# The MLP norm's factors by ScalarE's root and a Newton step, the input differences made inside the output projection, and that projection in finer steps of heads and tiles

## The chip, the cores and the metric

The kernel runs on one core of a Trainium2 chip. The metric is the device time of one execution in microseconds; the value shown is the median of three runs.

## The reference, cut to what matters

Four pre-norm residual layers on a stream of 16 learned meta positions and 512 frames, width 1024. Layer 0 and layer 3 mix tokens with a gated DeltaNet of 8 heads, layer 1 with differential attention of 8 heads, layer 2 with a Griffin RG-LRU block; each mixer ends in an output projection, and each layer is followed by a squared-ReLU MLP of inner width 4096:

```python
def rmsnorm(x, w):
    y = x * lax.rsqrt(jnp.mean(x * x, axis=-1, keepdims=True) + EPS)
    return y * w

def sq_relu_mlp(u, w1, w2):
    return jnp.square(jax.nn.relu(u @ w1)) @ w2

for layer in range(DEPTH):
    u = rmsnorm(h, norm_mix_w[layer])
    y = mixer(u)                      # heads' outputs o, then o @ w_out
    h = h + keep * y
    u = rmsnorm(h, norm_mlp_w[layer])
    h = h + keep * sq_relu_mlp(u, mlp_w1[layer], mlp_w2[layer])
```

## The kernel before, in words

The stream is kept transposed: eight tiles `h[0]` to `h[7]` of 128 features by 528 positions (512 positions from the last layer's output projection on). Every product of large matrices is made as three passes: a weight is split into `hi` and `lo`, an activation into `hi` and `lo`, and TensorE adds `hi·hi`, `hi·lo` and `lo·hi` in PSUM. Such a product runs over two halves of the positions (264 or 256 columns), so one 128 by 128 block of weights costs six matmuls. PSUM tiles come from two pools, `d` with three buffers and `c` with five.

**Weights.** They are streamed in units of eight blocks. `unit()` pops the next unit and prepares further ones: ScalarE casts `hi` (L305) and writes its negative to `lo` (L309), then a DMA that GpSimd issues (L310) adds the raw weights from memory to `lo`. The split tiles rotate through seven buffers.

**Background work.** The heads of a mixer are Python generators (`dn_core` and `dn_gate`, `da_core`) that are advanced between matmuls by `tick()`, by a hand-kept model time `self.now`; `drain(g, ...)` advances the model until these generators are done. The instructions so written are then ordered on each engine by the framework's own scheduler; each engine runs its order strictly, and waits at an instruction whose inputs are not there.

**Output projection** (`out_proj`, from L600). It multiplies the heads' outputs by `w_out` and adds the result into `h[d]` on VectorE (L612). For the DeltaNet and the attention it is called twice: once for heads 0 to 3 over all eight tiles `d`, then, after all heads are drained, for heads 4 to 7 over all eight tiles. In the second call every tile `d` is followed by `mlp_prep(d)`: ScalarE scales it by the norm's weight (L461) and casts `uh` (L462), VectorE makes `ul` (L463), ScalarE squares `h` (L429), and GpSimd adds the squares to `ssum` (L430; VectorE for `d` = 7).

**Start of the MLP** (`mlp`). `open()` starts the first two columns of the first MLP matrix, `w1p`, with input tiles 0 to 6, and leaves tile 7 for later. `norm_finish()` sums `ssum` over partitions with ten small matmuls, forms mean plus epsilon on VectorE (`ms`, L442), raises it to the power −1/2 on GpSimd (`rt`, L444), spreads the five columns over positions with ten more matmuls that read `rt`, and ScalarE copies the result to `rb` (L450), which scales everything that leaves PSUM afterwards. Then `mlp_combine(p)` for p = 0 to 3 makes, for each pair of input tiles, four differences of halves (VectorE, L477), two casts (ScalarE, L480 and L483) and two remainders (VectorE, L477). They are inputs of the seven-product scheme that computes the rest of the first MLP matrix (`w1_pair`, `prod`); the products named 11, 21 and 22 need no differences.

`norm_finish` is called nine times: before each of the four mixers, before each of the four MLPs, and at the end.

In `dn_core` the inverse of each head's triangular matrix passes through an image in memory (`dimg`); the tiles TM and TT are read back, and the head is held until the model time `t_img`, 4.0 us after the read was issued.

Of the kernel before, what the change touches and what calls it, by code (L numbers as in the profile page):

```python
# [11 lines left out]
AF = mybir.ActivationFunctionType  # L12
ALU = mybir.AluOpType
# [3 lines left out]
D = 1024  # L17
NT = 8
# [27 lines left out]
LO_ENG = {"w2": "vd", "lru_in": "vd", "lru_out": "vd", "lru_gate": "vd"}  # L46

PRODS = (11, 21, 2, 3, 4, 1, 22)
OUT_PARTS = {"dn_out": (4, 4), "da_out": (4, 4), "lru_out": (8,)}


def out_order(name):

    o, n0 = [], 0
    for n in OUT_PARTS[name]:
        o += [(d, k) for d in range(8) for k in range(n0, n0 + n)]
        n0 += n
    return o


def unit_list(layers=LAYERS):
# [85 lines left out]
class K:  # L147
    def __init__(self, ctx, tc, hT, wts, cols, bc, cst, onehot, relb, out, layers):
        self.tc, self.nc = tc, tc.nc
        nc = tc.nc  # L150
        self.wts, self.out, self.layers = wts, out, layers
        pool = lambda name, **kw: ctx.enter_context(tc.tile_pool(name=name, **kw))
        self.cp = pool("cp", bufs=1)
        self.rawp = pool("rawp", bufs=2)
        self.wp = pool("wp", bufs=7)
        self.sm = pool("sm", bufs=2)
        self.dps = pool("dps", bufs=3, space=PSUM)
        self.cps = pool("cps", bufs=5, space=PSUM)
        self.drp = pool("drp", bufs=2, space=DRAM)
        self.uid = 0  # L160

        def per(shape, name):
            return self.cp.tile(shape, F32, name=name)

        self.h = [per([128, T], f"h{d}") for d in range(NT)]
        self.u = [tuple(self.cp.tile([128, T], F32R, name=f"u{k}{d}") for k in "hl") for d in range(NT)]
        self.cols = per([128, NCOL], "cols")
        self.bc = per([128, NBC], "bc")
        self.cst = per([128, NCST], "cst")
        self.ssum = per([128, TP], "ssum")  # L170
        self.rb = per([128, TP], "rb")
        self.ones = per([128, 1], "ones")
        self.half = per([128, 1], "half")
        self.nhalf = per([128, 1], "nhalf")
        self.NS, self.NL = 34, 7
        self.sp = pool("sp", bufs=self.NS)
        self.lp = pool("lp", bufs=self.NL)
        self.slots = []
        self.rows = row_list(unit_list(layers))
        self.items = [(r, k) for r, us in enumerate(self.rows) for k in (range(7) if us[0][0] == "w1" else range(len(us)))]  # L180
        self.wq, self.wnext, self.raws, self.wahead = [], 0, {}, 0
        nc.scalar.dma_start(self.cols, cols)
        nc.sync.dma_start(self.h[0], hT[:, 0, :])
        self.raws[0] = self.rawp.tile([128, 2, 1024], F32, tag="raw", name="raw0")
        for d in range(1, NT):
            if d == 4:
                nc.sync.dma_start(self.raws[0][:, 0], wts[0, :, 0, :])
            nc.sync.dma_start(self.h[d], hT[:, d, :])
        if len(self.rows[0]) > 1:
            nc.sync.dma_start(self.raws[0][:, 1], wts[0, :, 1, :])  # L190
        nc.sync.dma_start(self.cst, cst)
        nc.sync.dma_start(self.bc, bc)
        nc.vector.memset(self.ssum, 0.0)
        nc.vector.memset(self.ones, 1.0)
        nc.vector.memset(self.half, 0.5)
        nc.vector.memset(self.nhalf, -0.5)
        self.ident = self.cst[:, CST["ident"]:CST["ident"] + 128]
        self.dimg = [self.drp.tile([2 * NC * (CB + 1), CB], F32, name=f"dimg{i}", bufs=1) for i in range(2)]
        self.dzero = False
        self.onehot_in, self.relb_in = onehot, relb  # L200
        self.bg = []
        self.fin = []
        self.wide = None
        self.dn_ = 0
        self.now = 0.0
        self.ready = {}
        self.hv, self.t0 = HV, 0
        self.lat = 1.6
        self.opened = {}
# [222 lines left out]
    def us(self):  # L432
        return self.u

    def norm_finish(self):

        nc = self.nc
        ps = self.psc()
        for c in range(NC):
            self.mmul(ps[:C, c:c + 1], lhsT=self.ssum[:, c * C:(c + 1) * C], rhs=self.ones, start=True, stop=True)  # L440
        ms = self.small([C, NC], "ms")
        nc.vector.tensor_scalar(ms, ps[:C, :NC], 1.0 / D, EPS, ALU.mult, ALU.add)  # L442
        rt = self.small([C, NC], "rt")
        nc.gpsimd.tensor_tensor(rt, ms, self.nhalf[:C].broadcast_to([C, NC]), ALU.pow)  # L444
        for c0, m in GR:
            pb = self.psc()
            for c in range(m):
                self.mmul(pb[:, c * C:(c + 1) * C], lhsT=rt[:, c0 + c:c0 + c + 1].broadcast_to([C, 128]),
                                 rhs=self.ident[:C, :C], start=True, stop=True)
            nc.scalar.copy(self.rb[:, c0 * C:(c0 + m) * C], pb[:, :m * C])  # L450
        return rt
# [123 lines left out]
    def mlp(self, l, next_prep, early=None):  # L575
        nc = self.nc
        self.open([("w1p", l, 0), ("w1p", l, 1)], self.us(), NT - 1)
        self.norm_finish()
        for p in range(NT // 2):
            self.mlp_combine(p)  # L580
        G = 32 // HG
        for g in range(G):
            xs = [] if g else self.w1_plain(l)
            for f in range(0 if g else 2, HG, 2):
                xs += self.w1_pair(l, g * HG + f, f == HG - 2)
            if g == 1 and early:
                self.spawn(early())
            self.wide = (0, 2, 4, 5, 7)
            self.open([("w2", l, d, g) for d in range(2)], xs, HG - 2)
            for d in range(NT):  # L590
                def ev(ps, t0, w):
                    h = self.h[d][:, t0:t0 + w]
                    nc.vector.tensor_tensor(h, h, ps, ALU.add)  # L593

                self.mm(("w2", l, d, g), xs, ev)
                if g == G - 1:
                    next_prep(d)
            self.wide = None

    def out_proj(self, name, slot, xs, l, part=None):  # L600

        nc = self.nc
        order = out_order(name)
        parts = OUT_PARTS[name]
        if part is None:
            part = len(parts) - 1
        n0, n = sum(parts[:part]), parts[part]
        if part == len(parts) - 1:
            self.ut, self.U = [], []
        for d in range(NT):  # L610
            def ev(ps, t0, w):
                nc.vector.tensor_tensor(self.h[d][:, t0:t0 + w], self.h[d][:, t0:t0 + w], ps, ALU.add)  # L612

            ws = []
            for k in range(n0, n0 + n):
                j, i = divmod(order.index((d, k)), 8)
                if i == 0:
                    self.ow = self.unit((name, slot, j))
                ws.append(tuple(x[:, i * 128:(i + 1) * 128] for x in self.ow))
            self.mmu(ws, [tuple(self.R(a) for a in xs[k]) for k in range(n0, n0 + n)], ev)  # L620
            if part == len(parts) - 1:
                self.mlp_prep(d, l * 8)


    def conv(self, x, y, wname, base, step, bias=None):
# [21 lines left out]
    def deltanet(self, slot, l, last):  # L647
# [45 lines left out]
        for h in range(8):  # L693
# [2 lines left out]
            hi, lo = self.get(True), self.get(True)  # L696
            xs.append((hi, lo))
            gates.append(self.spawn(self.dn_gate(heads[h], z, t, hi, lo), 0.7))
        n = 0
        for p, k in enumerate(OUT_PARTS["dn_out"]):  # L700
            n += k
            self.drain(*gates[:n])
            self.out_proj("dn_out", slot, xs, l, p)
        self.lat = 1.6

    def dn_beta(self, slot, xba, beta, ngc, negc, gd, tri):
# [68 lines left out]
    def dn_core(self, slot, l, h, cv, st, beta, ngc, negc, gd, mneg, ba):  # L775
# [97 lines left out]
        TM, TT = self.L(TMi, CB), self.L(TTi, CB)  # L873
        nc.sync.dma_start(TM[:CB], img(im, 0))
        nc.sync.dma_start(TT[:CB], img(im, NC * (CB + 1) * CB))
        t_img = self.now + 4.0
        yield 0.2

        vti = self.getl()
# [138 lines left out]
    def diffattn(self, slot, l, last):  # L1018
# [16 lines left out]
        for h in range(8):  # L1035
# [6 lines left out]
            self.mm(("da_in", slot, 8 + h), us, self.evac_rb(self.S(k)))  # L1042
            self.mm(("da_in", slot, 16 + h), us, self.evac_rb(self.S(v)))
            gens.append(self.spawn(self.da_core(h, xs, q, k, v, self.vs, nlam), 0.5))
        n = 0
        for p, k in enumerate(OUT_PARTS["da_out"]):
            n += k
            self.drain(*gens[:n])
            self.out_proj("da_out", slot, xs, l, p)

    def da_tiles(self, ts, q, k, E, Em, vt, on, so, nlam):
        nc = self.nc
# [235 lines left out]
def layout(i, layers=LAYERS):  # L1288
# [10 lines left out]
    for n, j, u in ((n, j, u) for n, us in enumerate(rows) for j, u in enumerate(us)):  # L1299
# [13 lines left out]
        elif u[0] == "w1p":  # L1313
            dst[:] = blk(i["mlp_w1"][u[1]], 0, u[2])
        elif u[0] == "w2":
            dst[:] = blk(i["mlp_w2"][u[1]], u[3], u[2])
        elif u[0] in OUT_PARTS:
            w = i[u[0][:-4] + "_w_out"][u[1]]
            for j, (d, k) in enumerate(out_order(u[0])[8 * u[2]:8 * u[2] + 8]):
                dst[:, j * 128:(j + 1) * 128] = w[k * 128:(k + 1) * 128, d * 128:(d + 1) * 128]  # L1320
        else:
            nm = {"dn_in": "dn_w_in", "da_in": "da_w_in", "lru_in": "lru_w_in"}[u[0]]
            dst[:] = blk(i[nm][u[1]], 0, u[2])
# [39 lines left out]
```

## Time and profile before

| what | value |
|---|---|
| median of three runs | 2815.55 us |
| lowest, highest | 2807.36 us, 2817.22 us |
| the profiled execution's own time | 2808.51 us |
| its span, first to last instruction | 2806.7 us |
| mean granted TensorE clock | 0.976 of full speed |
| TensorE busy | 2685.4 us, 96% of the span |
| VectorE busy | 1674.3 us, 60% |
| ScalarE busy | 1461.1 us, 52% |
| GpSimd busy | 720.2 us, 26% |

The profile is of one execution. Its times count from the first instruction. A wait is put down to what ended it. The granted clock has two levels, 1.0 (2.4 GHz) and 0.5 (1.2 GHz); a stretch of windows shows their mean.

### The profile page before, as it was taken

To read this page: it belongs to the slowest core of one execution; us is meant where nothing else is said; L and a number is where in the kernel's file an instruction comes from. 1 tells how busy PE (TensorE), PEld (TensorE's weight loads), DVE (VectorE), ACT (ScalarE), POOL (GpSimd) and SP (SyncE) were. 2 spreads that over 40 slices of the span, in tenths; PEclk is the share of its full clock that TensorE was granted. 3 is DMA by queue.
4 is the path that set the end of the run, shared out by engine and by line. 5 is a ranking of instruction groups with operands and counts; after the bars stand their busy time and mean duration, and the time that the engine had idled before them with its cause. 6 is when DMAs were issued, how large, how long until landed. Compare 5 with 4: busy or idle time off the path is not lost.

```text
span 2806.7 us, 54609 instructions
## 1 busy us (share of the span) xinstructions
PE 2685.4 (96%) x22080; PEld 2606.7 (93%) x22080; DVE 1674.3 (60%) x3841; ACT 1461.1 (52%) x3024; POOL 720.2 (26%) x984
## 2 busy tenths in 40 slices
PE   7899999999999999999999999999999999899997
PEld 7899898999998887999999999999999988799997
DVE  5755447656734445776566766776376553567763
ACT  4566555444545555543456854444566564544443
POOL 2655522101121112111122121111236453311112
PEclk9999999999999999999999999999999999999998
DMA  7755453354465443343454434433677454344333
GB/s 200 161 124 119 87 134 92 99 162 134 130 145 124 100 105 91 104 123 106 121 148 124 128 97 122 143 106 100 161 166 161 101 112 99 83 136 128 121 98 106
DMA packets 128866, 343.84 MB, mean 123 GB/s; under 512 B 72789, under 2 KB 73213, under 8 KB 103397
## 3 DMA queue, kind: packets, MB, share of 16 engines
q10 hardware_dynamic: 38496, 212.61, 22.0%
q0 software_dynamic: 28224, 102.77, 21.2%
q1 hardware_dynamic: 61892, 24.96, 3.7%
q8 instruction: 173, 2.83, 0.4%
q14 instruction: 81, 0.66, 0.1%
HBM read 331.99 MB, written 11.01 MB: 122 GB/s over the span
## 4 chain that ended last, share of the span: by engine, by line
PE 78%; issue 6%; DMA 5%; DVE 4%; POOL 4%; ACT 3%; DVEq 0%; ACTq 0%; POOLq 0%; SPq 0%
PE d L218 41%; PE c L218 35%; DMA lo<-in_wts_dram 2%; PE c L222 2%; POOL rt L444 1%; DVE op L307 1%; DMA s<-dimg 1%; DMA s<-gd 1%; POOL s L863 1%; DMA sa<-s 1%; POOL s L864 1%; ACT lo L309 0%; DMA gd<-l 0%; DVE l L539 0%; DMA dimg<-s 0%
## 5 line engine op out<-in xcount | busy, mean ns | idle before, releaser
L218 PE MATMUL c<-s,hi 128*128 128x264 f32 (+1 forms) x2816 | 522.0, 284 | 0.1
L218 PE MATMUL d<-uh,hi 128*128 128x264 f32 (+1 forms) x1584 | 468.5, 296 | 10.2 <-DVE s L642 10.1
L218 PE MATMUL d<-s,hi 128*128 128x264 f32 (+1 forms) x2432 | 467.9, 289 | 7.9 <-ACT s L400 2.0
L218 PE MATMUL d<-ul,hi 128*128 128x264 f32 (+1 forms) x1584 | 462.8, 292 | 0.0
L218 PE MATMUL d<-uh,lo 128*128 128x264 f32 (+1 forms) x1584 | 461.9, 292 | 0.4 <-DMA lo<-in_wts_dram 0.4
L218 PEld LDWEIGHTS c<-s,hi 128*128 128x128 f32 x2816 | 435.9, 188 | 1.4 <-issue 1.1
L310 POOL DMA_DIRECT2D lo<-in_wts_dram x196 | 173.9, 887 | 982.7 <-ACT lo L309 696.3
L218 PEld LDWEIGHTS d<-s,hi 128*128 128x128 f32 x2432 | 385.1, 192 | 13.6 <-issue 2.3
L218 PE MATMUL c<-s,lo 128*128 128x264 f32 (+1 forms) x1408 | 394.6, 284 | 1.9 <-DMA lo<-in_wts_dram 1.7
L309 ACT ACTIVATE lo<-hi 128x1024 fp32r<-128x1024 f32 x196 | 207.7, 1060 | 351.1 <-PE d L218 244.2
L305 ACT CAST hi<-raw 128x1024 fp32r<-128x1024 f32 x278 | 288.0, 1041 | 127.4 <-PE c L218 78.8
L218 PE MATMUL d<-s,lo 128*128 128x264 f32 (+1 forms) x1216 | 349.4, 288 | 3.6 <-DMA lo<-in_wts_dram 3.5
L218 PEld LDWEIGHTS d<-uh,hi 128*128 128x128 f32 x1584 | 306.4, 193 | 19.2 <-DVE s L642 13.7
L218 PEld LDWEIGHTS d<-uh,lo 128*128 128x128 f32 x1584 | 305.5, 193 | 5.2 <-issue 3.2
L218 PEld LDWEIGHTS d<-ul,hi 128*128 128x128 f32 x1584 | 306.0, 193 | 2.6 <-issue 1.6
L305 ACT CAST op<-raw 128x512 fp32r<-128x512 f32 x300 | 180.9, 619 | 168.7 <-PE d L218 100.3
L218 PEld LDWEIGHTS c<-s,lo 128*128 128x128 f32 x1408 | 263.5, 188 | 3.4 <-DMA lo<-in_wts_dram 3.1
L307 POOL TENSOR_TENSOR op<-raw,op 128x512 fp32r<-128x512 f32 x60 | 114.8, 1913 | 546.7 <-ACT op L305 407.0
L218 PEld LDWEIGHTS d<-s,lo 128*128 128x128 f32 x1216 | 232.9, 192 | 5.9 <-DMA lo<-in_wts_dram 4.2
L218 PE MATMUL d<-s,op 128*128 128x264 f32 (+1 forms) x1716 | 228.2, 284 | 0.0
L218 PEld LDWEIGHTS d<-s,op 128*128 128x128 f32 x1716 | 216.4, 188 | 0.0
L593 DVE TENSOR_TENSOR h<-h,c 128x264 f32<-128x264 f32 (+1 forms) x172 | 73.1, 425 | 229.3 <-PE c L218 228.9
(260 smaller groups left out, 5577.8 us busy)
## 6 DMA issues: line engine op xcount, KB each, us to landing
raw<-in_wts_dram ACTq DMA_DIRECT2D x197, 1024.0 KB
lo<-in_wts_dram POOLq DMA_DIRECT2D x196, 512.0 KB, 5.9
s<-dimg SPq DMA_DIRECT2D x32, 245.0 KB
sa<-s SPq DMA_DIRECT2D x16, 245.0 KB
s<-gd ACTq DMA_DIRECT2D x14, 265.0 KB
vs<-vd SPq DMA_DIRECT2D x8, 327.5 KB
h<-in_hT_dram SPq DMA_DIRECT2D x8, 264.0 KB
s<-vs SPq DMA_DIRECT2D x8, 264.0 KB
```

Of the source, the lines that this page charges most:

```text
L218: return self.nc.tensor.matmul(out, lhsT=lhsT, rhs=rhs, start=start, stop=stop)
L222: return self.nc.tensor.transpose(out, in_, ident)
L305: nc.scalar.copy(hi, src)
L307: lo_eng.tensor_tensor(lo, src, hi.bitcast(F32), ALU.subtract)
L309: nc.scalar.activation(lo, hi.bitcast(F32), AF.Copy, scale=-1.0)
L310: nc.gpsimd.dma_start(lo, dram, accum_op=ALU.add)
L444: nc.gpsimd.tensor_tensor(rt, ms, self.nhalf[:C].broadcast_to([C, NC]), ALU.pow)
L593: nc.vector.tensor_tensor(h, h, ps, ALU.add)
L863: nc.gpsimd.tensor_tensor(t, bt[:, j, j + 1:, None].broadcast_to([NB, r, j]), X[:, None, j, :j].broadcast_to([NB, r, j]), ALU.mult)
L864: nc.gpsimd.tensor_tensor(X[:, j + 1:, :j], X[:, j + 1:, :j], t, ALU.subtract)
```

## The change

1. The four calls of `norm_finish` ahead of the MLPs take a new path (`root=True`): ScalarE takes the square root of mean plus epsilon straight from PSUM, VectorE forms −1/2 of mean plus epsilon, takes the reciprocal of the root and refines it by one Newton step (three more small operations). The other five calls keep GpSimd's power.
2. `mlp_combine(0)`, `(1)` and `(2)` are called inside the output projection, after tiles 1, 3 and 5 are finished; only `mlp_combine(3)` stays behind `norm_finish`.
3. `out_proj` is one call that runs through a list of steps (tile, first head, end of heads), and before each step drains only the heads that the step needs. For the DeltaNet and the attention the list is: all tiles with heads 0 to 3, tiles 0 to 3 with heads 4 to 6, tiles 0 to 3 with head 7, tiles 4 to 7 with heads 4 to 7. `mlp_prep(d)` follows the step that ends with head 7. The blocks of `w_out` are stored in that order. For the RG-LRU the list is all heads per tile, as before.
4. In `dn_core` head 0 is held 5.5 us of model time, instead of 4.0, after the read of its image.

```diff
+HEADS4 = [(d, 0, 4) for d in range(8)] + [(d, 4, 7) for d in range(4)] + [(d, 7, 8) for d in range(4)] + [(d, 4, 8) for d in range(4, 8)]
+OUT_STEPS = {"dn_out": HEADS4, "da_out": HEADS4, "lru_out": [(d, 0, 8) for d in range(8)]}
...
-    def norm_finish(self):
+    def norm_finish(self, root=False):
...
+        rt = self.small([C, NC], "rt")
         ms = self.small([C, NC], "ms")
-        nc.vector.tensor_scalar(ms, ps[:C, :NC], 1.0 / D, EPS, ALU.mult, ALU.add)
-        rt = self.small([C, NC], "rt")
-        nc.gpsimd.tensor_tensor(rt, ms, self.nhalf[:C].broadcast_to([C, NC]), ALU.pow)
+        if root:
+
+            sq = self.small([C, NC], "sq")
+            nc.scalar.activation(sq, ps[:C, :NC], AF.Sqrt, scale=1.0 / D, bias=self.eps[:C])
+            nc.vector.tensor_scalar(ms, ps[:C, :NC], -0.5 / D, -0.5 * EPS, ALU.mult, ALU.add)
+            nc.vector.reciprocal(rt, sq)
+            nc.vector.tensor_tensor(sq, rt, rt, ALU.mult)
+            nc.vector.tensor_tensor(sq, sq, ms, ALU.mult)
+            nc.vector.scalar_tensor_tensor(rt, sq, 1.5, rt, ALU.add, ALU.mult)
+        else:
+            nc.vector.tensor_scalar(ms, ps[:C, :NC], 1.0 / D, EPS, ALU.mult, ALU.add)
+            nc.gpsimd.tensor_tensor(rt, ms, self.nhalf[:C].broadcast_to([C, NC]), ALU.pow)
...
     def mlp(self, l, next_prep, early=None):
...
-        self.norm_finish()
-        for p in range(NT // 2):
-            self.mlp_combine(p)
+        self.norm_finish(True)
+        self.mlp_combine(NT // 2 - 1)
...
-    def out_proj(self, name, slot, xs, l, part=None):
+    def out_proj(self, name, slot, xs, l, gens=()):
...
-        for d in range(NT):
+        for d, k0, k1 in OUT_STEPS[name]:
+            self.drain(*gens[:k1])
...
-            self.mmu(ws, [tuple(self.R(a) for a in xs[k]) for k in range(n0, n0 + n)], ev)
-            if part == len(parts) - 1:
+            self.mmu(ws, [tuple(self.R(a) for a in xs[k]) for k in range(k0, k1)], ev)
+            if k1 == 8:
                 self.mlp_prep(d, l * 8)
+                if d % 2 == 1 and d < NT - 1:
+                    self.mlp_combine(d // 2)
...
-        n = 0
-        for p, k in enumerate(OUT_PARTS["dn_out"]):
-            n += k
-            self.drain(*gates[:n])
-            self.out_proj("dn_out", slot, xs, l, p)
+        self.out_proj("dn_out", slot, xs, l, gates)
...
-        t_img = self.now + 4.0
+        t_img = self.now + (4.0 if h else 5.5)
```

The attention's caller is changed like the DeltaNet's.

## Rows read from the trace of the kernel before

**Rows 1.** The page's first line.

```profile
span 2806.7 us, 54609 instructions
```

**Rows 2.** Who TensorE waited for, whole span: us in total, times, longest us.

```profile
PE c L218 <- POOL rt L444: 21.9, 5, 5.5
PE c L218 <- DMA s<-dimg: 13.5, 6, 4.1
...
PE c L218 <- DMA lo<-in_wts_dram: 8.3, 6, 2.6
...
PE d L218 <- DVE h L612: 0.9, 2, 0.6
```

**Rows 3.** Timeline of TensorE, first MLP start and final norm: start, us, [idle before].

```profile
447.59 2.47 PE L218 MATMUL c<-cst,rt 106*128 106x106 f32 x10 [5.51 <-POOL rt L444]
...
2792.66 2.47 PE L218 MATMUL c<-cst,rt 106*128 106x106 f32 x10 [1.53 <-POOL rt L444]
```

**Rows 4.** Timeline of GpSimd, the same two places.

```profile
439.69 7.85 POOL L444 TENSOR_TENSOR rt<-ms,nhalf 106x5 f32<-106x5 f32 x1 [10.85 <-DVE ms L442]
...
2791.41 1.19 POOL L444 TENSOR_TENSOR rt<-ms,nhalf 106x5 f32<-106x5 f32 x1 [6.61 <-DVE ms L442]
```

**Rows 5.** Windows, the four MLP starts: busy us, granted clock, DMA.

```profile
447.60:452.40 4.80, 4.80 (x22) 4.80 (x23) 2.15 (x5) 1.29 (x3) 1.17 (x1) 0.50 0.00 0
1135.20:1141.00 5.80, 5.79 (x26) 5.79 (x27) 2.15 (x5) 1.90 (x5) 1.20 (x1) 0.50 0.00 0
1673.50:1678.00 4.50, 4.50 (x21) 4.50 (x22) 2.15 (x5) 1.19 (x3) 1.13 (x1) 0.50 0.02 4
2452.70:2456.20 3.50, 3.50 (x17) 3.50 (x18) 1.56 (x4) 1.46 (x4) 1.15 (x1) 0.52 0.00 0
```

**Rows 6.** Windows around the last head of layers 1 and 3.

```profile
1083.90:1092.50 8.60, 4.35 (x20) 2.70 (x19) 3.25 (x14) 1.93 (x8) 2.95 (x3) 0.71 0.52 153
1092.50:1097.60 5.10, 5.10 (x24) 5.10 (x25) 2.20 (x5) 2.92 (x5) 0.00 (x0) 0.50 0.00 0
2400.00:2409.00 9.00, 3.42 (x17) 2.31 (x15) 2.29 (x9) 2.31 (x6) 2.47 (x2) 0.78 0.31 54
2409.00:2412.00 3.00, 3.00 (x15) 3.00 (x16) 1.26 (x3) 1.45 (x3) 0.00 (x0) 0.52 0.00 0
```

**Rows 7.** Windows, layer 0: heads 4 to 7 of the projection, then the opening.

```profile
397.00:430.00 33.00, 30.41 (x234) 29.76 (x233) 15.28 (x28) 21.74 (x34) 12.81 (x11) 0.95 0.68 156
430.00:442.00 12.00, 12.00 (x101) 11.87 (x100) 11.89 (x27) 6.57 (x13) 2.31 (x1) 1.00 0.01 1
```

**Rows 8.** VectorE's groups by shape, 403 to 448 us: busy, mean ns.

```profile
L612 DVE TENSOR_TENSOR h<-h,d 128x264 f32<-128x264 f32 x16 | 6.7, 426 | 14.7 <-PE d L218 14.6
L477 DVE TENSOR_TENSOR s<-l,s 128x528 fp32r<-128x528 f32 x6 | 4.1, 698 | 0.0
...
L477 DVE TENSOR_TENSOR l<-s,l 128x264 f32<-128x264 f32 x8 | 3.1, 425 | 0.0
```

**Rows 9.** ScalarE's groups, whole span.

```profile
L1162 ACT ACT_TABLE_LOAD x8 | 10.3, 1283 | 0.1
...
L480 ACT CAST s<-l 128x528 fp32r<-128x528 f32 (+1 forms) x16 | 10.1, 629 | 16.1 <-DVE l L477 16.1
...
L795 ACT ACTIVATE eg<-eg 106x5 f32<-106x5 f32 x16 | 3.2, 200 | 6.6 <-DVE eg L794 6.6
```

**Rows 10.** A small reciprocal on VectorE, whole span.

```profile
L820 DVE RECIPROCAL cj<-nk 106x5 f32<-106x5 f32 x16 | 2.9, 182 | 0.1
```

**Rows 11.** The sums of squares, and the operation on VectorE beside them: ns min/median/max.

```profile
L430 POOL TENSOR_TENSOR ssum<-ssum,l x51: 1252/1317/1838, 8.7 to 2783.5; 128x528 f32<-128x528 f32 x39, 128x512 f32<-128x512 f32 x12
...
L463 DVE TENSOR_TENSOR ul<-s,uh x32: 683/1242/1487, 406.8 to 2439.5; 128x528 fp32r<-128x528 f32 x24, 128x512 fp32r<-128x512 f32 x8
```

**Rows 12.** The weights' `lo` transfers issued at L310, 397 to 425 us.

```profile
DMA to landing us min/median/max: 5.7/7.5/8.5
```

More of the change, by code (lines that the diff above doesn't have):

```diff
@@ L48 @@
 PRODS = (11, 21, 2, 3, 4, 1, 22)
-OUT_PARTS = {"dn_out": (4, 4), "da_out": (4, 4), "lru_out": (8,)}
+HEADS4 = [(d, 0, 4) for d in range(8)] + [(d, 4, 7) for d in range(4)] + [(d, 7, 8) for d in range(4)] + [(d, 4, 8) for d in range(4, 8)]
+OUT_STEPS = {"dn_out": HEADS4, "da_out": HEADS4, "lru_out": [(d, 0, 8) for d in range(8)]}
 def out_order(name):
[L54 to L58, printed above, removed]
+    return [(d, k) for d, k0, k1 in OUT_STEPS[name] for k in range(k0, k1)]
 def unit_list(layers=LAYERS):
@@ L173, in __init__ @@
         self.half = per([128, 1], "half")
+        self.eps = per([128, 1], "eps")
         self.nhalf = per([128, 1], "nhalf")
@@ L195, in __init__ @@
         nc.vector.memset(self.half, 0.5)
+        nc.vector.memset(self.eps, EPS)
         nc.vector.memset(self.nhalf, -0.5)
@@ L598, in mlp @@
             self.wide = None
-    def out_proj(self, name, slot, xs, l, part=None):
+    def out_proj(self, name, slot, xs, l, gens=()):
         nc = self.nc
[L603 to L607, printed above, removed]
-        if part == len(parts) - 1:
-            self.ut, self.U = [], []
-        for d in range(NT):
+        self.ut, self.U = [], []
+        n = 0
+        for d, k0, k1 in OUT_STEPS[name]:
+            self.drain(*gens[:k1])
             def ev(ps, t0, w):
@@ L614, in out_proj @@
             ws = []
-            for k in range(n0, n0 + n):
-                j, i = divmod(order.index((d, k)), 8)
+            for k in range(k0, k1):
+                j, i = divmod(n, 8)
                 if i == 0:
@@ L619, in out_proj @@
                 ws.append(tuple(x[:, i * 128:(i + 1) * 128] for x in self.ow))
-            self.mmu(ws, [tuple(self.R(a) for a in xs[k]) for k in range(n0, n0 + n)], ev)
-            if part == len(parts) - 1:
+                n += 1
+            self.mmu(ws, [tuple(self.R(a) for a in xs[k]) for k in range(k0, k1)], ev)
+            if k1 == 8:
                 self.mlp_prep(d, l * 8)
+                if d % 2 == 1 and d < NT - 1:
+                    self.mlp_combine(d // 2)
     def conv(self, x, y, wname, base, step, bias=None):
@@ L1044, in diffattn @@
             gens.append(self.spawn(self.da_core(h, xs, q, k, v, self.vs, nlam), 0.5))
[L1045 to L1049, printed above, removed]
+        self.out_proj("da_out", slot, xs, l, gens)
     def da_tiles(self, ts, q, k, E, Em, vt, on, so, nlam):
@@ L1316, in layout @@
             dst[:] = blk(i["mlp_w2"][u[1]], u[3], u[2])
-        elif u[0] in OUT_PARTS:
+        elif u[0] in OUT_STEPS:
             w = i[u[0][:-4] + "_w_out"][u[1]]
```

## The prediction

> **What bounds the kernel now.** I read the page first: over a span of 2806.7 us [rows 1] TensorE is almost never idle, so only places where it waits, or runs at the lower of its two clock levels, can give time back. The table of TensorE's waits says where. It loses 21.9 us in five waits for GpSimd's power `rt`, 13.5 us in six waits for the image `dimg`, 8.3 us in six waits for a weight's `lo` [rows 2]. One of the five waits for `rt` is the final norm, 1.53 us, which keeps its code [rows 3]; the other four are the MLP starts, 21.9 − 1.5 = 20.4 us, the first of them 5.51 us [rows 3].
>
> GpSimd's timeline shows why they are long. The same 106 by 5 power takes 1.19 us at the final norm, where VectorE is idle, and 7.85 us at the first MLP start [rows 4], where VectorE runs back to back: in the 12 us before, it is busy 11.89 us [rows 7], with weights and with the 24 operations of the four `mlp_combine`. The power comes out when VectorE's queue runs dry.
>
> The windows then show a second price. After each of the four waits the granted clock is 0.5: for 4.8, 5.8, 4.5 and 3.5 us [rows 5]. In a full-speed stretch a matmul takes 12.00/101 = 0.119 us, in the first of these 4.80/22 = 0.218 us [rows 5, 7], so half of each stretch is lost: 18.6/2 = 9.3 us. The norm at the MLP starts costs 20.4 + 9.3 = 29.7 us.
>
> The same windows show the last head. In layer 1 TensorE is busy 4.35 of 8.6 us, and then runs 5.1 us at clock 0.50; in layer 3 it is busy 3.42 of 9.0 us, and then 3.0 us at 0.52 [rows 6]. That is 4.25 + 2.55 + 5.58 + 1.45 = 13.8 us. In layer 0 nothing of this size stands there: 397 to 430 us has 30.41 us of work in 33 [rows 7], and most of the rest is a weight's `lo`.
>
> **The change part by part.**
>
> *The root.* The power goes from GpSimd, and with it the blocking by VectorE. In its place stand ScalarE's root and four dependent operations on VectorE. Nearest rows: a 106 by 5 activation 0.20 us [rows 9], a 106 by 5 reciprocal 0.18 us [rows 10]; with four such steps and the hand-overs the chain is 0.2 + 4 × 0.2 + some 0.3, about 1.3 us, as long as the unblocked power. TensorE has cover for it: the tile 7 of both opened columns, 12 matmuls of 0.119 us, and one or two products that need no differences, 12 matmuls each, so 2.9 to 4.3 us. Left alone, the wait would be gone. New is an activation table: other functions follow in the next mixer, so four loads for the root and three for the way back, 1.28 us each [rows 9]. The three on the way back stand at a mixer's start, beside matmuls, and ScalarE is busy for 52% of the span; I count them as nothing, 3.8 us if that cover is gone. The four in front of the root can be done while ScalarE waits for the sums: nothing if ScalarE is free, 5.1 us if it is not. I take nothing here and give the load a rival.
>
> The Trainium skill speaks against this edit: ScalarE: Activation LUTs, section "Table sets: the hidden batching unit", puts root and exponential in different sets and advises against alternating them, at about 2.7 us a load; seven loads would be 18.9 us by that figure. The trace's own load is less than half of it.
>
> *The differences.* One `mlp_combine` is four operations of 0.425 us and two of 0.698 us on VectorE [rows 8], 3.1 us, and two casts of 0.63 us on ScalarE [rows 9]. Three of the four move ahead of the norm, 9.3 us of VectorE and 3.8 us of ScalarE. The work is the same; what counts is whether it fits there.
>
> *The finer steps.* The number of matmuls is unchanged. Tiles 0 to 3 with heads 4 to 6 are 4 × 3 × 6 = 72 matmuls, 8.6 us, that now stand ahead of the wait for head 7; before, only the first nine of them did. The additional 7.5 us exceeds the 4.25 and 5.58 us of idle time, so both waits should close and the clock should hold: 13.8 us back. The price: 8 more additions into `h` per layer, 0.43 us of VectorE each [rows 8], in a stretch where it is half idle, so nothing, and 3.4 us a layer if it is not; and the three-buffer pool `d`: each step with head 7 alone frees a buffer only after an addition, and two additions take 0.85 us against six matmuls of 0.119 us, 0.71 us. Lower end 0, since three buffers cover some of it; upper end 2 us a layer. The nearest row is 0.9 us in two waits for these additions [rows 2]. I take 1 us for each of three layers.
>
> *The burst.* Here is what the change costs. Before, the eight `mlp_prep` were spread over 192 matmuls, 23 us. Now the first can start only with head 7's own steps, and the last 24 + 96 = 120 matmuls, 14.3 us, hold all eight. Add the opening, 84 matmuls, 10.0 us: 24.3 us from the first `mlp_prep` to the sums. Into them must go ScalarE's 21.7 us of before [rows 7], weights among them, and 3.8 us of casts, 25.5 us; and VectorE's 15.3 us [rows 7] and 9.3 us of differences, 24.6 us. Both are full. So the last squares will come late. Over this lies the conflict with GpSimd: `ul` on VectorE goes from 0.68 to 1.49 us, and a sum on GpSimd from 1.25 to 1.84 us, when they meet [rows 11]. I expect the sums 2 us late in layers 0, 1 and 3, with 1 us more for the clock, and 1 us in layer 2, where each tile has 48 matmuls and no burst exists: 10 us. Bounds: 0, and the whole of the old loss in three layers, about 23 us.
>
> So the norm gives back 29.7 − 10 = 19.7 us and the last head 13.8 − 3 = 10.8 us.
>
> *Weights.* With the stalls gone, units are consumed faster, while a `lo` takes up to 8.5 us to land [rows 12] and its issue stands in GpSimd's queue behind the sums. Three of the six waits for `lo`, up to 2.6 us [rows 2], stand at the openings of `w1p`. Bounds: all three go (6.6 us gained), or each doubles (6.6 us lost). I take 2 us lost.
>
> *Head 0.* 1.5 us more of model time puts a dozen other matmuls ahead of the first wait for `dimg`, the longest, 4.1 us [rows 2]. Taken: 1.5 us gained; bounds 0 and 4.1 us. The other heads' waits stay.
>
> Sum: 19.7 + 10.8 − 2 + 1.5 = 30.0 us. The profiled execution, 2808.5 us (the span and 1.8 us around it), would go to 2778.5 us; it lies 7.0 us under the median shown, so the median 2815.5 would go to 2785.5.
>
> **The rivals.**
>
> *The sums come late.* The burst is worse than I take it: GpSimd's sums of squares and VectorE's differences hold each other up as the power and the differences did [rows 4, 11], VectorE waits for the sixth sum before it can add the last, and TensorE waits about 5 us in layers 0, 1 and 3, with the clock lost again. Then these three keep some 23 us and the gain is 6.7 + 10.8 − 2 + 1.5 = 17 us: 2798.5. For it: both engines are full by the count above. Against it: VectorE's waits let GpSimd through, and VectorE's additions from PSUM have one operand in SBUF only. By the Trainium skill (SBUF — State Buffer, section "SBUF: two separate sides") the pair of ports that both use is locked for a whole instruction, and a two-input operation of VectorE takes part; the trace's 1.19 against 7.85 us agrees.
>
> *The table load stands in the chain* of each of the four norms: 4 × 1.28 = 5.1 us less gain, 2790.5. For it: ScalarE is full at that point. Against it: where a root waits for other data the load can run ahead.
>
> *Everything closes*, the burst included: 29.7 + 13.8 + 1.5 = 45 us, 2770.5. For it: the scheduler may put the third set of differences behind the sums.
>
> *The weights take it back.* Each of the three openings waits a whole landing, 8.5 us, with half a clock stretch of 2.4 us, against 2.2 us now: 3 × 8.7 = 26 us less than the waits of today, so 32 − 26 = 6 us gained: 2809.5. For it: 0.68 of the transfer engines' time is already taken there [rows 7].
>
> *Slower:* ScalarE's queue blocks. The squares (L429) and the differences share seven rotating buffers: the square of tile 5 needs a buffer of the first differences, that of tile 7 one of the second. If ScalarE stands there until VectorE's remainders are done, the casts of the next weights stand behind it, and TensorE waits for those. It decides when TensorE loses over 30/3 = 10 us a layer more than I took; at 15 us a layer the time is 2830. For it: the full engines. Against it: the remainders are only two operations of 0.7 us behind their cast.
>
> **How the numbers follow.** Chances: the forecast, 2785.5 us, 0.42; sums late 0.20; load in the chain 0.10; everything closes 0.14; weights 0.09; slower 0.05. The range 2765 to 2806 holds the forecast, the load, nearly all of "everything closes" and of "sums late", some 0.82. Half a per cent is 14 us, about what a measurement of this kernel can tell from no change. Faster by more: 0.42 + 0.10 + 0.14 + 0.12 of the late sums + 0.02 of the weights = 0.80. Within: the rest of those, 0.15. Slower: 0.05.
>
> **What would show it.** Right: no wait for `rt` of over 2 us at the MLP starts, no clock of 0.5 behind them, no idle time over 1 us before head 7's matmuls in layers 1 and 3. Burst: a wait for `ssum` or `uh`, `ul` at the openings. Load: `ACT_TABLE_LOAD` between the last sum and the root. Weights: waits for `lo` over 3 us at `w1p`. The prediction would be wrong if TensorE's total of waits fell by less than 10 us, or if matmuls elsewhere met new waits that this sum does not name.

## The result, and the profile after

The changed kernel takes 2780.15 us, the median of four runs (2772.98 to 2784.34), against 2815.54 for the kernel before in the same comparison: a ratio of 0.9877, with a 95% interval of 0.9848 to 0.9907. That is 35.4 us, where 30.0 were forecast. The profiled execution took 2782.64 us. First its page's first line, which answers to [rows 1]:

```profile
span 2780.8 us, 54669 instructions
```

Next, who TensorE waited for over the whole span (us in total, times, longest us), which answers to [rows 2]. Lines have moved: the root's last step is L451, `ul` L473, the differences L487, the casts of the differences L490 and L493.

```profile
PE c L218 <- DMA s<-dimg: 14.5, 6, 4.8
...
PE d L218 <- DMA lo<-in_wts_dram: 4.9, 4, 2.3
PE c L218 <- DVE ul L473: 4.6, 7, 1.1
PE c L218 <- DMA lo<-in_wts_dram: 4.1, 3, 1.8
...
PE c L218 <- POOL rt L454: 1.5, 1, 1.5
...
PE c L218 <- ACT uh L472: 0.7, 1, 0.7
PE c L218 <- DVE rt L451: 0.6, 1, 0.6
```

Of 21.9 us for `rt` the final norm's 1.5 and 0.6 at one MLP start are left. New are 5.3 us for `ul` and `uh`. The wait for `dimg` has not become shorter.

The MLP starts are best compared by how many matmuls TensorE gets done in a fixed stretch. The windows below are 22 us long, from 14 us ahead of the first copy into `rb` to 8 us behind it, for layers 0 to 3. The columns are start and end, length, busy time and instructions of TensorE, its weight load, VectorE, ScalarE and GpSimd, then granted clock, DMA share and GB/s. The kernel before:

```profile
435.20:457.20 22.00, 16.49 (x119) 16.28 (x118) 17.05 (x37) 10.87 (x21) 9.09 (x2) 0.84 0.15 48
1122.90:1144.90 22.00, 16.49 (x113) 16.28 (x112) 15.75 (x35) 10.14 (x20) 8.47 (x2) 0.77 0.05 8
1661.10:1683.10 22.00, 17.46 (x129) 17.25 (x128) 16.84 (x37) 10.97 (x21) 7.87 (x2) 0.84 0.09 26
2440.20:2462.20 22.00, 17.14 (x135) 16.94 (x134) 15.59 (x35) 10.72 (x21) 8.37 (x2) 0.92 0.15 48
```

The changed kernel:

```profile
427.90:449.90 22.00, 19.47 (x159) 18.92 (x158) 21.72 (x44) 15.19 (x28) 2.50 (x3) 1.00 0.14 48
1115.30:1137.30 22.00, 20.54 (x168) 20.02 (x167) 21.97 (x46) 15.29 (x28) 1.46 (x2) 1.00 0.15 49
1650.70:1672.70 22.00, 22.00 (x186) 22.00 (x185) 18.02 (x37) 13.30 (x25) 1.79 (x2) 1.00 0.14 49
2417.60:2439.60 22.00, 20.88 (x166) 20.68 (x165) 19.21 (x41) 14.58 (x27) 6.32 (x3) 0.92 0.15 48
```

Before, 119 + 113 + 129 + 135 = 496 matmuls; after, 679. At 0.119 us each, 183 more are 21.8 us of work, out of the 25.9 us between the two profiled executions (2808.51 and 2782.64 us). But only layer 2 is full (186 matmuls in 22 us), the layer whose projection has no finer steps. VectorE is now the full engine there: in layers 0 and 1 it was busy for 17.05 and 15.75 us of 22, now for 21.72 and 21.97.

The timeline of the changed kernel at the first MLP start shows what is late there:

```profile
429.99 0.63 ACT L490 CAST s<-l 128x528 fp32r<-128x528 f32 x1 [2.65 <-DVE l L487]
...
430.63 0.39 PE L218 MATMUL c<-ul,hi 128*128 128x264 f32 x1 [0.76 <-DVE ul L473]
...
432.77 0.63 ACT L493 CAST s<-l 128x528 fp32r<-128x528 f32 x1 [0.28 <-DVE l L487]
433.31 1.36 ACT L471 ACTIVATE s<-h,cols 128x528 f32<-128x528 f32 x2
...
434.58 1.15 ACT L472 CAST uh<-s 128x528 fp32r<-128x528 f32 x2
...
435.25 0.39 PE L218 MATMUL c<-uh,hi 128*128 128x264 f32 x1 [0.74 <-ACT uh L472]
...
435.74 1.28 ACT L446 ACT_TABLE_LOAD   x1
...
437.04 0.27 ACT L446 ACTIVATE sq<-c,eps 106x5 f32<-106x5 f32 x1
437.16 0.39 PE L218 MATMUL c<-ul,hi 128*128 128x264 f32 x1 [1.04 <-DVE ul L473]
...
437.72 0.17 DVE L448 RECIPROCAL rt<-sq 106x5 f32<-106x5 f32 x1
...
438.78 0.17 DVE L451 SCALAR_TENSOR_TENSOR rt<-sq,rt 106x5 f32<-106x5 f32 x1
```

ScalarE stands 2.65 us at a cast of differences that VectorE has not made yet, and scales two more tiles (L471) behind the next such cast. So `uh` and `ul` come late, and TensorE waits for them, 0.76, 0.74 and 1.04 us. The table load does stand between the sums and the root here, but the columns already opened cover it; in layers 2 and 3 it ran ahead of the sums, and the root then waited 1.96 and 1.37 us for them. From the reciprocal to the last step of the root 1.2 us pass.

At the last head of layer 3 two windows and the timeline answer to the lower half of [rows 6]:

```profile
2390.00:2395.50 5.50, 2.24 (x9) 1.54 (x9) 1.93 (x7) 1.57 (x3) 1.56 (x2) 0.65 0.93 269
2395.50:2398.60 3.10, 3.10 (x15) 3.10 (x16) 2.10 (x6) 1.48 (x3) 0.00 (x0) 0.52 0.00 0
```

```profile
2390.94 1.13 PE L222 MATMUL c<-cst,l 106*128 106x106 f32 x5 [1.72 <-DVE l L989]
2394.03 1.01 PE L218 MATMUL d<-s,hi 128*128 128x256 f32 x3 [1.96 <-ACT s L400]
2395.41 0.58 PE L218 MATMUL d<-s,hi 128*128 128x256 f32 x1 [0.36 <-POOL s L401]
```

It has not closed: 1.72 + 1.96 + 0.36 = 4.0 us of waits where 5.58 us were idle, and 3.1 us at clock 0.52 behind them. The three waits are for head 7's normalized output `l`, for the `hi` of its split and for the `lo`.

### The profile page after: what moved, and what is told of

It is laid out like the page before. It is cut to its first block, busy times and chain, and to the rows that moved or that the text cites. A ratio compares the mean times of both kernels' runs of the same rounds, so it can differ in the third digit from the quotient of the medians.

```text
span 2780.8 us, 54669 instructions
## 1 busy us (share of the span) xinstructions
PE 2676.9 (96%) x22080; PEld 2597.1 (93%) x22080; DVE 1694.4 (61%) x3882; ACT 1470.8 (53%) x3035; POOL 707.8 (25%) x980
## 3 DMA queue, kind: packets, MB, share of 16 engines
q0 software_dynamic: 28224, 102.77, 21.8%
## 5 line engine op out<-in xcount | busy, mean ns | idle before, releaser
L218 PE MATMUL d<-uh,lo 128*128 128x264 f32 (+1 forms) x1584 | 468.2, 296 | 0.4 <-DMA lo<-in_wts_dram 0.4
L310 POOL DMA_DIRECT2D lo<-in_wts_dram x196 | 173.6, 886 | 1002.7 <-ACT lo L309 706.5
L307 POOL TENSOR_TENSOR op<-raw,op 128x512 fp32r<-128x512 f32 x60 | 121.9, 2032 | 579.4 <-ACT op L305 363.4
```

What stands on the lines that cost most here:

```text
L218: return self.nc.tensor.matmul(out, lhsT=lhsT, rhs=rhs, start=start, stop=stop)
L307: lo_eng.tensor_tensor(lo, src, hi.bitcast(F32), ALU.subtract)
L310: nc.gpsimd.dma_start(lo, dram, accum_op=ALU.add)
```

## The experiments

Every kernel below was timed beside the kernel before, in three groups of four; the median of before was 2813.9, 2812.3 and 2812.6 us in them. The four parts of the change were first undone one at a time.

**The power kept** (finer steps, differences in the projection, 5.5 us stay):

```diff
-        self.norm_finish(True)
+        self.norm_finish()
```

> The changed kernel with one part undone: the four MLP norms go back to GpSimd's power; the differences stay within the projection, the finer steps stay. Theory A (the power is held up as long as VectorE has work queued, and weights alone keep it full): TensorE waits for rt again at the four MLP starts, some 3 us each with a clock of 0.5 behind, so 12 to 20 us above the changed kernel's median of 2780. Rival B (only the 24 operations of the differences held the power up; three quarters of them are now done earlier): the power takes 1.2 to 2 us as at the final norm, rt waits stay under 1 us each, and the time is the changed kernel's within 3 us; the root would then buy nothing.

Measured: 2771.66 us (2769.70 to 2779.50), ratio 0.9851 [0.9833, 0.9869]. Theory B, though the median lies 8.5 us under the changed kernel's and not within 3; the second measurement of that kernel below puts it at 3.3 us. At the four MLP starts the power on GpSimd now takes 1.93, 2.55, 1.20 and 1.37 us, and `rt` costs TensorE 0.6 us there. The root buys nothing that could be measured.

**All differences behind the norm** (root, finer steps, 5.5 us stay):

```diff
-        self.mlp_combine(NT // 2 - 1)
+        for p in range(NT // 2):
+            self.mlp_combine(p)
...
-                if d % 2 == 1 and d < NT - 1:
-                    self.mlp_combine(d // 2)
```

> The changed kernel with all four sets of differences again behind the norm; root and finer steps stay. Theory A (ScalarE's queue, where casts of differences wait for VectorE, is what makes the last tiles' uh and ul late): the waits for ul and uh, 5.3 us in the changed kernel, fall under 2 us, and the time is 0 to 5 us below the changed kernel's; the move is then worth nothing by itself once the root is there. Rival B (the differences behind the norm are too late for the first seven-product columns): new waits for x, y, x2 or y2 at the first w1 columns of each MLP, 2 to 3 us each, and 5 to 12 us above.

Measured: 2796.38 us (2792.20 to 2801.79), ratio 0.9941 [0.9925, 0.9957], 16 to 21 us over the changed kernel. Theory A's waits for `ul` did go, but the time rose. In layers 1 and 2 it is as rival B says: the first products that need differences wait for them, 4.1 and 3.9 us. In layers 0 and 3, which neither theory had, TensorE waits for the root's own `rt`, 7.1 and 5.3 us:

```profile
PE c L218 <- DVE rt L451: 12.4, 2, 7.1
...
PE d L218 <- DVE s L487: 5.6, 3, 2.2
...
PE d L218 <- ACT s L490: 2.3, 2, 1.9
```

Together these are 20.3 us, as much as the 20.4 us for the power before. With all differences in VectorE's queue, something that TensorE needs comes late at each of the four starts.

**Two passes of four heads** (root, differences in the projection, 5.5 us stay):

```diff
-HEADS4 = [(d, 0, 4) for d in range(8)] + [(d, 4, 7) for d in range(4)] + [(d, 7, 8) for d in range(4)] + [(d, 4, 8) for d in range(4, 8)]
+HEADS4 = [(d, 0, 4) for d in range(8)] + [(d, 4, 8) for d in range(8)]
```

> The changed kernel with the output projection of layers 0, 1 and 3 in two passes of four heads again; root and differences stay. Theory A (the added matmuls cover the last head, in part only, since its last steps come some 3 us later): idle time and low clock before head 7's matmuls return in layers 1 and 3, and the time is 4 to 9 us above the changed kernel's. Rival B (full cover, as forecast): 10 to 14 us above. Rival C (what the last head gains is paid again where all eight preparations fall into the last 120 matmuls): the same time within 2 us, with fewer waits for uh and ul at the MLP starts.

Measured: 2772.97 us (2770.03 to 2775.24), ratio 0.9856 [0.9838, 0.9874]. Theory C: without the finer steps nothing is lost (2.0 us under the second median of the changed kernel below), although the wait for `l` at the last head of layer 3 is back at 2.8 us. The four windows at the MLP starts hold 186 + 167 + 186 + 192 = 731 matmuls, where the changed kernel has 679.

**Head 0's image at 4.0 us**:

```diff
-        t_img = self.now + (4.0 if h else 5.5)
+        t_img = self.now + 4.0
```

> The changed kernel with head 0's image planned 4.0 instead of 5.5 us after its loads. Theory A: the first wait for dimg grows again, layers 0 and 3 lose 0.5 to 1.5 us each, the time is 1 to 3 us above the changed kernel's, which a comparison of medians can hardly tell; the trace's waits for dimg in layers 0 and 3 tell it. Rival B: other work is moved into the stretch and the wait only changes its place: waits for dimg as in the changed kernel, the same time.

Measured: 2778.31 us (2770.86 to 2779.47), ratio 0.9870 [0.9851, 0.9890]. No difference to be seen in the time. The trace has four waits for `dimg`, 9.7 us, against 14.5 in six, but that is scatter too: over all traces here they are 9.7 to 16.4 us in the six with 4.0 us, and 10.4 to 16.1 us in the eight with 5.5. The longer hold gains nothing that can be seen.

Then the parts were put one at a time into the kernel before, the first of them beside the changed kernel on the same chip.

**The changed kernel again:**

> The changed kernel as it is, beside the next three on one chip. Both theories: 2772 to 2784, as in its first four runs. It says whether the 8 us by which the kernel with the power kept was faster is more than the scatter of runs: theory A (the root costs something by itself) wants it above 2776, rival B (root and power are worth the same once the differences are gone) wants it at 2770 to 2775.

Measured: 2774.97 us (2768.61 to 2778.40), ratio 0.9864 [0.9848, 0.9881]. This is the upper edge of rival B's range. What the kernels with the power, the two passes and the 4.0 us differ from it by lies within the scatter. Its second profile has 158 + 185 + 186 + 169 = 698 matmuls in the four windows.

**The differences alone** (power, two passes, 4.0 us as before):

```diff
     def mlp(self, l, next_prep, early=None):
...
-        for p in range(NT // 2):
-            self.mlp_combine(p)
+        self.mlp_combine(NT // 2 - 1)
...
                 self.mlp_prep(d, l * 8)
+                if d % 2 == 1 and d < NT - 1:
+                    self.mlp_combine(d // 2)
```

> The kernel before with one part of the change alone: three of the four sets of differences move into the output projection. Power, two passes of four heads and 4.0 us for every image stay. Theory A (the move of the differences is the whole gain): 2768 to 2776, as fast as the changed kernel or a little faster; waits for rt at the MLP starts under 1 us each although the power stays. Rival B (the parts add up, the root and the finer steps carry the forecast's 10.8 us and more): 2785 to 2800.

Measured: 2779.14 us (2776.99 to 2781.87), ratio 0.9885 [0.9869, 0.9901]. Theory A, 33.2 us under the kernel before, 3 us slower than it expected. Its four windows:

```profile
432.60:454.60 22.00, 22.00 (x186) 22.00 (x185) 20.37 (x37) 13.69 (x27) 3.84 (x3) 1.00 0.15 48
1110.60:1132.60 22.00, 21.62 (x179) 21.26 (x178) 21.56 (x37) 12.61 (x24) 4.53 (x3) 1.00 0.14 49
1642.00:1664.00 22.00, 22.00 (x186) 22.00 (x185) 17.40 (x33) 11.71 (x23) 3.00 (x3) 1.00 0.14 48
2411.80:2433.80 22.00, 22.00 (x191) 22.00 (x190) 21.50 (x41) 14.03 (x27) 4.93 (x4) 1.00 0.15 49
```

TensorE is full in three of them and nearly so in layer 1, with the power still there: 742 matmuls, 246 more than before, 29.3 us. The norm at the MLP starts was counted at 29.7 us; this one part gives all of it back. The timeline of GpSimd and VectorE at the first start answers to [rows 4]:

```profile
443.26 0.17 DVE L453 TENSOR_SCALAR ms<-c 106x5 f32<-106x5 f32 x1 [0.25 <-PE c L218]
443.34 0.70 DVE L487 TENSOR_TENSOR s<-l,s 128x528 fp32r<-128x528 f32 x1
443.51 1.59 POOL L454 TENSOR_TENSOR rt<-ms,nhalf 106x5 f32<-106x5 f32 x1 [12.54 <-DVE ms L453]
445.16 1.75 DVE L307 TENSOR_TENSOR op<-raw,op 128x512 fp32r<-128x512 f32 x1 [1.12 <-ACT op L305]
```

One operation of the differences stands beside the power; then VectorE pauses for 1.12 us, and the power ends in that pause, after 1.59 us instead of 7.85. By the Trainium skill (SBUF — State Buffer, section "SBUF: two separate sides") the shared ports are locked for a whole instruction, and VectorE's operations with two SBUF inputs take part; these rows agree.

**The root alone** (differences behind the norm, two passes, 4.0 us):

```diff
-        self.norm_finish()
+        self.norm_finish(True)
```

> The kernel before with the root alone: four sets of differences stay behind the norm. Theory A (four dependent steps in VectorE's queue, with operations of the differences between them, wait as long as one blocked power): waits for rt of 4 to 7 us stay at two or more of the four MLP starts, and the time is 2800 to 2818. Rival B (the forecast's own account: with the power gone its wait is gone): no wait for rt over 1 us, 2785 to 2795.

Measured: 2815.97 us (2810.37 to 2823.79, 12 runs), ratio 1.0013 [1.0002, 1.0024]. Theory A. The windows at layers 0 to 3 hold 116, 122, 121 and 110 matmuls, 469 where 496 were before. TensorE waits for `rt` in layers 0 and 3, 6.4 and 7.0 us. In layers 1 and 2 it waits 0.6 us and nothing for `rt`, but 3.5 and 3.9 us for differences:

```profile
PE c L218 <- DVE rt L451: 14.0, 3, 7.0
...
PE d L218 <- DVE s L487: 5.6, 3, 2.2
...
PE d L218 <- ACT s L490: 1.8, 2, 1.4
```

That is 21.4 us in all, where the power cost 20.4. VectorE's timeline at the first start, with the start of TensorE's `rt` matmuls:

```profile
441.81 0.18 DVE L448 RECIPROCAL rt<-sq 106x5 f32<-106x5 f32 x1
...
443.50 1.50 DVE L487 TENSOR_TENSOR l<-s,s 128x264 f32<-128x264 f32 x1
444.92 0.15 DVE L449 TENSOR_TENSOR sq<-rt 106x5 f32<-106x5 f32 x1
...
447.16 0.15 DVE L450 TENSOR_TENSOR sq<-sq,ms 106x5 f32<-106x5 f32 x1
...
449.40 0.15 DVE L451 SCALAR_TENSOR_TENSOR rt<-sq,rt 106x5 f32<-106x5 f32 x1
...
449.70 0.52 PE L218 MATMUL c<-cst,rt 106*128 106x106 f32 x1 [6.43 <-DVE rt L451]
```

From the reciprocal to the last step 7.6 us pass, of which the steps themselves are 0.18 + 3 × 0.15 = 0.63. In the gaps stand differences and weights: the scheduler put them between the dependent steps, and VectorE runs its order strictly. In layer 0 the chain on VectorE is about as long as the blocked power was (7.85 us).

**The differences one step later** (else as the differences alone):

```diff
-                if d % 2 == 1 and d < NT - 1:
-                    self.mlp_combine(d // 2)
+                if d in (2, 4, 7):
+                    self.mlp_combine((2, 4, 7).index(d))
```

> As the kernel with the differences alone, but each set comes one step later: the first after tile 2, the second after tile 4, the third after tile 7, so that no cast of theirs stands ahead of the scaling of tiles 6 and 7. Theory A (casts that wait for VectorE hold up the preparation of the last tiles): waits for ul and uh at the MLP starts, 4.7 us, fall under 2 us, and the time is 2 to 5 us under the kernel with the differences alone. Rival B (the order in the queues hangs on when data are there, not on where the code stands): the same waits, the same time within 3 us. Rival C (the third set comes too late and stands between the sums and the power): waits for rt of 1 to 3 us are back, 2 to 6 us slower.

Measured: 2796.68 us (2792.19 to 2799.79), ratio 0.9941 [0.9927, 0.9955], 17.5 us over the differences alone. Rival C in layer 0, where the power takes 4.62 us and TensorE waits 4.4 us for `rt` again. The waits for `ul` and `uh` that theory A aims at are those of other kernels: the trace of the differences alone has none, so this run does not test A. More than C had lies in waits for weights, 7.1 us over those of the differences alone (12.8 us in both pools):

```profile
PE c L218 <- DMA lo<-in_wts_dram: 11.2, 4, 4.5
...
PE c L218 <- POOL rt L454: 6.0, 2, 4.4
```

Half of the gain goes when the sets of differences move one or two tiles back. In layers 1 to 3 the windows are as full as with the differences alone (186, 186 and 191 matmuls), so the loss there is not the norm's. Why `lo` is late in layers 1 and 3 (4.5 and 3.7 us) was not followed up.

**The finer steps alone** (power, differences behind the norm, 4.0 us):

```diff
-OUT_PARTS = {"dn_out": (4, 4), "da_out": (4, 4), "lru_out": (8,)}
+HEADS4 = [(d, 0, 4) for d in range(8)] + [(d, 4, 7) for d in range(4)] + [(d, 7, 8) for d in range(4)] + [(d, 4, 8) for d in range(4, 8)]
+OUT_STEPS = {"dn_out": HEADS4, "da_out": HEADS4, "lru_out": [(d, 0, 8) for d in range(8)]}
```

> The kernel before with the finer steps alone: power, differences behind the norm and 4.0 us for every image stay. Theory A (the last head's cover is worth what the forecast took, and is paid again only where the differences stand in the same stretch): 2793 to 2804, 8 to 19 us under the kernel before. Rival B (the finer steps are worth nothing anywhere): 2808 to 2816.

Measured: 2816.70 us (2800.96 to 2826.45, 12 runs), ratio 1.0013 [0.9997, 1.0029]. Rival B. The waits ahead of head 7 shrink as little as in the changed kernel (in layer 3 for `l` from 2.8 to 1.7 us, for ScalarE's `s` 2.0 as before), and two waits for `lo` of 3.7 and 3.8 us stand inside the MLPs of layers 1 and 3. At the MLP start of layer 3 the power takes 2.25 us here, TensorE does not wait for it, and the window holds 178 matmuls; the other three still wait 6.2, 6.5 and 4.5 us.

**Two finer tiles instead of four**, the power kept:

```diff
-HEADS4 = [(d, 0, 4) for d in range(8)] + [(d, 4, 7) for d in range(4)] + [(d, 7, 8) for d in range(4)] + [(d, 4, 8) for d in range(4, 8)]
+HEADS4 = [(d, 0, 4) for d in range(8)] + [(d, 4, 7) for d in range(2)] + [(d, 7, 8) for d in range(2)] + [(d, 4, 8) for d in range(2, 8)]
```

> The changed kernel with the power kept, and with two tiles in finer steps where it has four: 36 matmuls of heads 4 to 6 stand ahead of the wait for head 7, and the eight preparations spread over 156 matmuls, not 120. Theory A (the finer steps pay at the MLP start, by late ul and uh, what they save at the last head): the waits for ul and uh fall from 4.7 us to under 2 us, half of the cover at the last head stays, 2764 to 2771. Rival B (the last head's wait comes back as a whole): 2772 to 2780, as with two passes or a little slower.

Measured: 2785.91 us (2783.90 to 2794.35), ratio 0.9909 [0.9892, 0.9926]. Neither: slower than with four such tiles and than with none. The MLP starts did become fuller (174, 173, 186 and 190 matmuls, 723), but in layer 3 the 2.8 us for `l` are back with 2.9 us for a `lo`. The rest of the loss lies elsewhere, and its cause stays open.

**The `lo` of the first `w1p` column on VectorE**, with two finer tiles, and with two passes:

```diff
-            dram = None if r < 2 or LO_ENG.get(key[0], "dd")[k] == "v" else self.wts[r, :, k, :]
+            dram = None if r < 2 or LO_ENG.get(key[0], "dd")[k] == "v" or key[0] == "w1p" and key[2] == 0 else self.wts[r, :, k, :]
```

> As the kernel with two fine tiles, and the lo of the first w1p column of each layer is made by one subtraction on VectorE, 1.4 us for 128 by 1024, not by a transfer that adds. Theory A (after the change the largest wait at an MLP start is for this lo, 1 to 3 us): the waits for lo fall by 3 to 6 us over the four layers, the time by 2 to 5 us. Rival B (VectorE is full there, so 1.4 us more a layer come out as later ul, ssum or rt): the same time within 2 us, or 2 to 6 us slower.

> Two passes of four heads, the power kept, the differences within the projection, 5.5 us for head 0's image, and the lo of the first w1p column on VectorE. Theory A: without the finer steps VectorE has more room in this stretch, the lo is not late and nothing else is: 2766 to 2772, the fastest with the kernel of two fine tiles. Rival B (the late lo only covered for a late rt): waits for rt of 1 to 2 us appear, 2772 to 2778.

Measured: 2786.53 us (2782.74 to 2787.86), ratio 0.9903 [0.9888, 0.9918], and 2776.41 us (2770.71 to 2781.87), ratio 0.9870 [0.9851, 0.9889]. Rival B in both, by the time: in the second the waits for `lo` in the `c` pool nearly go (1.1 us in two), those in the `d` pool are 8.9 us in seven, and the time is that of the others.

So five other kernels that have three sets of differences in the projection, behind tiles 1, 3 and 5, and four fine tiles or none lie between 2771.7 and 2779.1 us, the changed kernel at 2775.0 and 2780.2, with overlapping intervals. None was shown to beat it.

## Why the prediction was right, and where not

The time was forecast well, 30.0 us for 35.4. The parts of the sum were not; that the total came out is in good part luck. Of the forecast's own signs two held, no wait for `rt` over 2 us at the MLP starts and no low clock behind one (in layer 3 a wait of 1.12 us for `ul` has 3.3 us at 0.50 to 0.53 behind it); the third, no idle time over 1 us before head 7's matmuls, did not (1.72 and 1.96 us in layer 3, 1.51 in layer 1).

**The norm, 19.7 us.** The size holds: 21.8 us in the windows of the changed kernel. The cause does not. "The power goes from GpSimd, and with it the blocking by VectorE", and "left alone, the wait would be gone": left alone, the root gave nothing (ratio 1.0013). Its chain was costed as durations and hand-overs, some 1.3 us, and not by what the scheduler puts between them: 7.6 us in layer 0 with the differences beside it, 1.2 us once they are gone. And where the root was early, the products that need the differences waited in its place. The 29.7 us came back through the part that had no term of its own in the sum, "the work is the same; what counts is whether it fits there". What counted was that 18 of the 24 operations, 9.3 us of VectorE, no longer stood beside the norm. The prediction had read the right row, that the power ends when VectorE's queue runs dry, and did not ask which of the two edits empties that queue.

**The burst, 10 us of that term.** Shown in place and nearly in size. The changed kernel holds 679 and 698 matmuls in the four windows of its two profiles, 681 with the power kept and 644 with 4.0 us for the image; the kernels with two passes hold 731 and 742 (718 with the `lo` on VectorE). Against the first two that is 33 to 98 fewer, 3.9 to 11.7 us, and none of it in layer 2 (186 in all of them). It appears as waits for `uh` and `ul`, as named, not for `ssum`. The cause was named only in part. "Both are full" came out for VectorE, 21.72 of 22 us in layer 0, and not for ScalarE, 15.19 of 22, since the count put the work of a stretch of 33 us into 24.3: ScalarE stands at casts whose differences are not made. That these casts cause the lateness was read from the timeline and is not shown; the one run that moved them started from a kernel that has no such waits.

**The last head, 10.8 us.** This step failed. "The additional 7.5 us exceeds the 4.25 and 5.58 us of idle time, so both waits should close and the clock should hold": in layer 3 4.0 us of waits stayed where 5.58 were idle, in layer 1 2.3 us (1.51 for head 7's `hi`, 0.78 for its `lo`) where 4.25 were, and the clock fell behind them, to 0.52 in layer 3 and to a mean of 0.72 over 6 us in layer 1. Alone the finer steps gave nothing (ratio 1.0013), and undoing them lost nothing. Two things show in the traces. The work put ahead took 1.1 us off the wait for `l` in layer 3 and all 2.4 us in layer 1, but nothing off the split of head 7's output, whose `hi` and `lo` stand directly ahead of its matmuls. And head 7 itself came later: from the projection's first addition to the last product of its recurrence 32.8 us before, 36.0 after, because its steps are issued by model time between the added matmuls. The second was seen, not tried apart.

**Weights, −2 us.** TensorE's waits for `lo` were 8.3 + 3.9 us before, 4.1 + 4.9 after, 11.8 in the second profile: nothing lost, up to 3 us gained.

**Head 0, +1.5 us.** Not there: `dimg` waits of 14.5 and 16.1 us against 13.5, the longest 4.8 us against 4.1. Over all traces the two holds cannot be told apart.

**The rivals.** The table load stands in the chain in layer 0 and in part in layer 1, as rival two said, and costs nothing, as its undoing shows (power kept: not slower). The trace has 17 loads before and 24 after: seven were added, as forecast, four for the root and three on the way back in the next mixers (at 788.67, 1478.04 and 2028.21 us), each 1.283 us. The Trainium skill (ScalarE: Activation LUTs, section "Table sets: the hidden batching unit") counts two loads for an exponential followed by a root, at about 2.7 us each; this trace agrees with the count, and a load takes half of that time. "Everything closes" is what the differences alone do at the MLP starts. ScalarE's blocked queue, the slower rival, came in another form and at about a tenth of its price: ScalarE stands at casts, but for differences that are not made and not for buffers, and what TensorE waits for is `uh` and `ul` and not the next weights, 5.3 us in all, not 15 a layer.

Not settled: the root alone and the finer steps alone give nothing, yet both together, with differences behind the norm and the 5.5 us, gave 17.5 us, and not at the MLP starts, whose windows hold 474 matmuls there. And the two profiled executions of the changed kernel lie 25.9 and 33.4 us under that of the kernel before, which is itself 7 us under its median; the windows explain 21.8 and 24.0 of these. The stage of the attention alone went from 326.4 us to 327.8 in one profile of the changed kernel and to 321.1 in the other, so single profiles cannot divide the remainder.

## What to carry to other kernels

When two edits aim at one wait, ask of each alone what stands in the queue that the wait ends behind: here moving 18 operations of VectorE away (with six casts of ScalarE) gave everything, and replacing the blocked operation by a dependent chain in the same queue gave nothing. Cost a chain of small dependent steps by what a scheduler may put between them, not by their durations. Cover placed ahead of a serial tail helps only up to the tail's last hand-over, and it may make the tail itself later (seen here, not tried apart).

## What was not expected of the hardware

A 106 by 5 power on GpSimd, 1.19 us alone and 7.85 beside a VectorE that never paused, came down to 1.59 us with a single pause of 1.12 us in VectorE's work: what it needs is not an idle engine but a gap.

The lower clock came as early as before, though the idle stretch was shorter: in the same two places, the matmuls behind the wait for `l` and the wait behind them, it was 0.81 and then 0.50 in both kernels. At the last head of layer 3 the changed kernel's windows are:

```profile
2390.90:2392.10 1.20, 1.13 (x5) 0.73 (x5) 0.68 (x4) 0.51 (x1) 0.00 (x0) 0.81 1.03 300
2392.10:2394.00 1.90, 0.00 (x0) 0.00 (x0) 0.69 (x1) 1.07 (x3) 0.00 (x0) 0.50 1.02 306
```

Here the clock fell behind the first wait, of 1.72 us, and was at 0.50 throughout the second. The 4.0 us of waits are followed by 3.1 us at 0.52, as the 5.58 us of idle time were before by 3.0 us. Shortening such a stretch without closing it gave no clock back here. The length of a single wait does not tell what follows: in the same trace the clock is 0.53 behind the wait of 1.12 us for `ul` that ended at 2425.66 us, and 1.00 behind a wait of 2.27 us for a `lo` that ended at 1604.42 us.
